# GpSimd's element work ahead of the feed-forward part handed to VectorE and ScalarE, and second buffers for two small tables

## The chip, the core and the metric

The kernel runs on one core of a Trainium2 chip. The time is the device time of one execution in microseconds; the profile is of one execution. The engines are named as in the profile: PE (TensorE matrix multiplies; PEld its weight loads), DVE (VectorE), ACT (ScalarE), POOL (GpSimd), and SP, which issues the DMAs. Each engine works through its own queue in order, and waits on semaphores of the others.

## The reference

One transformer layer over 2048 tokens of width 1024, all in float32:

```
mod = silu(c) @ w_ada + b_ada            # six vectors: shift, scale, gate, twice
h   = rmsnorm(x) * (1 + scale1) + shift1
p   = h @ w_in
y_a = spatial gating of 128-token chunks (gelu, rmsnorm, causal 128x128 mixing)
y_b = 6 stick-breaking heads: weight = sigmoid(z) * product of sigmoid(-z) behind it
y_c = 6 dilated heads (strides 1, 4, 16; 129 offsets), rotary q and k, softmax;
      the three groups are scaled by a softmax over their log sums
x   = x + (1 + gate1) * (concat(y_a, y_b, y_c) @ w_out)
h   = rmsnorm(x) * (1 + scale2) + shift2
up  = causal depthwise convolution, width 3, of h @ w_up
x   = x + (1 + gate2) * ((silu(gate half) * val half) @ w_down)
out = rmsnorm(x) * g_final
```

## The kernel before

Products are made exact enough by splitting each operand into a rounded high part and the remainder: `split` (L88) casts the source to the high tile (L70, L72 or L74, by engine) and subtracts (L78) for the low tile. Every matrix product is then three PE products (high by high, high by low, low by high). So each weight piece that lands from memory as `wraw` passes through one cast to `whi` and one subtraction to `wlo` before PE can use it; the same holds for normed activations (`ln_tmp`, `hh`, `hl`; in the feed-forward part `gh`, `gl`), for rotated queries and keys (`rot`), and for the output weights (`woraw`, `wo_hi`, `wo_lo`) and the concatenated heads (`yraw`, `yh`, `yl`).

The tokens are worked on in two chunks of 1024. A text of tokens, `ORDER`, says in which order the units are written: projections of the queries and keys, of the values, of the gating part, stick-breaking heads (`st`), dilated heads (`dil`), the vectors from `w_ada`, the output projection (`op`, `oa`). Units marked with a tilde are worked off piece by piece between the blocks of stick-breaking heads. The tile framework then orders all instructions by a simulated timeline of its own, so a change of an instruction's engine also changes the order that the other engines get.

Which engine does a split's cast or subtraction, or one of the other element operations, is read from the table `ENGINES`: a letter for each site (a ACT, v DVE, p POOL), or a string of letters taken in turn. `whi` and `wlo` are the input weights' casts and subtractions (`whi0` and `wlo0` those of the opening stretch), `hlo0` and `hlo` the activations' low parts, `rot1` to `rotlo` the rotary steps, `sgu1` to `sgulo` the gating steps, `wolo`, `ysc`, `ylo` those of the output projection. The site `beta` (a product on the way from DVE's scan to PE's transposes) is POOL's in both kernels, and so are the feed-forward sites `wulo`, `wdm`, `wdlo`, `gv`, `ghi`, `glo`.

A block of a stick-breaking head passes PE (`z`), ACT (two sigmoids, L539 and L540), DVE (scan `excl`, L545), POOL (`beta`), PE (transposes `tr`), ACT (`wh`), DVE (`wl`, L78) and PE again (`av`). A dilated head writes scores' maxima and sums into the table `stat` and the negated maxima into `mx`; at its end `stat` is stored to memory. `BUFS` gives each tag its number of buffers; tags that it does not name have one, as `stat` and `mx` here:

```
nc.vector.tensor_tensor_reduce(e[:, j, ks], z[:, j, ks], self.mask[:, ks], 0.125, -3.0e38,
                               ALU.add, ALU.max, stat[:, blk, 0:1])
...
self.load(sd.rearrange("(p r) s -> p r s", r=16), stat)
```

In the opening stretch DVE sums the rows of `w_ada` into `ada_acc` (L185, L187), quarter by quarter; after each quarter PE sums over partitions (`ada_ps`), DVE finishes the columns `cols` (L179 to L181), and only then can the activations of that quarter be normed and multiplied.

Of the kernel before, what the change touches and what calls it, by code (L numbers as in the profile page):

```python
# [43 lines left out]
class Kernel:  # L44
# [16 lines left out]
    def engine(self, site):  # L61

        turns = ENGINES.get(site, site)
        n = self.turn[site] = self.turn.get(site, -1) + 1
# [790 lines left out]
    def run(self):  # L855
        tc, nc, i = self.tc, self.nc, self.i
        self.constants()
        self.ps = _Bufs(self.pool("ps", space=PSUM), BUFS)
        self.p1 = _Bufs(self.pool("p1"), BUFS)
        self.pa = _Bufs(self.pool("pa", side="right"), BUFS)  # L860
        dr = self.dr
# [185 lines left out]
        for c, order in enumerate(ORDER):  # L1047
            u = units(c, hT[c])
            for token in order.split():
# [48 lines left out]
                elif what == "rel":  # L1098
                    finish()
                    self.p1.release()  # L1100
                    self.ps.release()
                    self.ps = _Bufs(self.pool("ps2", space=PSUM), {**BUFS, "gm": 2, "z": 3})
                    self.po = _Bufs(self.pool("po"), BUFS)
                elif what == "free":
                    finish()
                    self.pa.release()
                    self.pw = _Bufs(self.pool("pw", side="right"), BUFS)
                    self.pn = _Bufs(self.pool("pn", side="right"), BUFS)
# [41 lines left out]
        self.cp.release()  # L1150


ENGINES = {"whi0": "a", "wlo0": "pppv", "lnt0": "a", "hlo0": "pppv", "lnt": "va", "lnx00": "avv", "lnx01": "aav", "lnx10": "v", "lnx11": "v", "lnx": "va", "hlo": "pvv", "whi": "v", "wlo": "pvv", "qkhi": "avv", "qklo": "v", "cqk": "a", "rot1": "ppv", "rot2": "pv", "rot3": "v", "rothi": "aav", "rotlo": "pvv", "sgu1": "pv", "sgu2": "p", "sguhi": "ap", "sgulo": "ppv", "ya": "aaav", "fold": "a", "beta": "p", "whi_s": "a", "whi_d": "avv", "wom": "v", "wohi": "aav", "wolo": "pv", "ysc": "pv", "yhi": "av", "ylo": "pv", "wuhi": "v", "wulo": "pvv", "wdm": "p", "wdhi": "av", "wdlo": "ppv", "upc": "av", "gv": "pppv", "ghi": "ap", "glo": "ppv", "vhi": "av", "vlo": "v", "uc": "v"}

BUFS = {"gm": 3, "z": 2, "tr": 2, "av": 1, "wraw": 2, "whi": 3, "wlo": 3, "s8": 3, "cs": 2, "tmp2": 2, "khat": 3, "vhat": 2, "q": 2, "beta": 4, "excl": 3, "wh": 2, "wl": 2, "fold": 1, "ys": 1, "x4": 2, "yraw": 2, "ysc": 4, "yh": 2, "yl": 2, "xo": 3, "wuraw": 4, "wul": 3, "wuh": 3, "wdraw": 2, "fx": 2, "up": 3, "dn": 5, "wdh": 2, "wdl": 2, "upc": 3, "cv": 3, "gh": 4, "gl": 4, "fs": 4, "fry": 2, "frr": 2}

WOUT = 6
EARLY = (0, 1, 5, 6, 7)
# [39 lines left out]
```

## Time and profile before

| | us |
|---|---|
| median of 3 runs | 2798.26 (2794.84 to 2798.34) |
| the profiled execution | 2798.01 |
| its span, first to last instruction | 2796.3 |
| busy in the span: PE, DVE, ACT, POOL | 2641.1, 2122.0, 983.0, 1043.6 |

About the first 1200 us are the part ahead of the feed-forward part, with some 1400 us as the point from which nearly all work is feed-forward. An engine's idle time costs something only where PE ends up waiting for it. [...]

### The profile page before, as it was taken

How to read it: one execution, taken by the hardware profiler on the slowest of the kernel's cores; microseconds unless marked ns; L12 is line 12 of the kernel's file. 1: busy time of each engine (PE TensorE's matmuls, PEld its weight loads, DVE VectorE, ACT ScalarE, POOL GpSimd, SP SyncE). 2: the span in 40 equal slices, each digit the busy share in tenths (PEclk: the TensorE clock that was granted, in tenths of full speed). 3: DMA queues.
4: the chain of work that ended last, by engine and by line, in shares of the span. 5: the costliest groups of instructions: out<-in, count | busy, mean ns of one | idle time of the engine just before them, and what ended most of it. 6: DMA issues, size and time to landing. Idle time of an engine off the chain costs nothing.

```text
span 2796.3 us, 36851 instructions
## 1 busy us (share of the span) xinstructions
PE 2641.1 (94%) x13430; PEld 2210.9 (79%) x13430; DVE 2122.0 (76%) x3188; ACT 983.0 (35%) x1842; POOL 1043.6 (37%) x995
## 2 busy tenths in 40 slices
PE   6989899799988999999999999999998999999998
PEld 5878888788966777877788888888877888888886
DVE  5586878666588898855877777778788778777776
ACT  5244433333455677633221222121362112112114
POOL 3163413230037555423433334433444343333323
PEclk9999999899998999999999999999999999999999
DMA  7645485869665333186111111111232111111111
GB/s 236 194 126 165 153 267 163 216 169 232 169 167 158 99 91 95 54 270 241 59 45 46 46 46 53 49 50 53 68 106 98 53 50 49 48 50 46 46 38 61
DMA packets 305298, 309.38 MB, mean 111 GB/s; under 512 B 65517, under 2 KB 245597, under 8 KB 305117
## 3 DMA queue, kind: packets, MB, share of 16 engines
q1 hardware_dynamic: 305116, 307.02, 37.0%
q8 instruction: 107, 1.75, 0.3%
q14 instruction: 75, 0.61, 0.1%
HBM read 232.36 MB, written 68.30 MB: 108 GB/s over the span
## 4 chain that ended last, share of the span: by engine, by line
PE 61%; DVE 13%; DMA 9%; ACT 4%; issue 3%; POOL 1%; SPq 1%; DVEq 0%; POOLq 0%; ACTq 0%
PE up L93 11%; PE up L94 11%; PE up L92 11%; PE dn L94 5%; PE dn L92 5%; PE dn L93 5%; DVE excl L545 3%; PE gmv L342 3%; DMA wada<-in_w_ada_dram 2%; PE av L565 2%; DMA wraw<-in_w_in_dram 1%; DVE wl L78 1%; SPq L83 1%; PE tr L554 1%; PE op L102 1%
## 5 line engine op out<-in xcount | busy, mean ns | idle before, releaser
L92 PE MATMUL up<-gh,wuh 128*128 128x512 f32 x1408 | 553.5, 393 | 2.1 <-ACT gh L260 2.1
L94 PE MATMUL up<-gh,wul 128*128 128x512 f32 x1408 | 555.2, 394 | 0.0
L93 PE MATMUL up<-gl,wuh 128*128 128x512 f32 x1408 | 555.0, 394 | 0.0
L829 DVE TENSOR_TENSOR acc<-dn,acc 128x512 f32<-128x512 f32 x688 | 441.2, 681 | 102.3 <-PE dn L94 101.6
L787 DVE SCALAR_TENSOR_TENSOR cv<-upc,cw,cv 128x512 f32<-128x512 f32 x352 | 338.5, 962 | 104.7 <-ACT cv L785 101.5
L78 POOL TENSOR_TENSOR beta<-beta,excl 128x127 f32<-128x127 f32 (+2 forms) x240 | 258.4, 1080 | 290.6 <-DVE excl L545 259.9
L92 PEld LDWEIGHTS up<-gh,wuh 128*128 128x128 f32 x1408 | 265.1, 188 | 62.1 <-ACT gh L260 2.3
L93 PEld LDWEIGHTS up<-gl,wuh 128*128 128x128 f32 x1408 | 265.4, 189 | 61.4 <-issue 0.2
L94 PEld LDWEIGHTS up<-gh,wul 128*128 128x128 f32 x1408 | 265.2, 188 | 60.0 <-issue 0.2
L92 PE MATMUL dn<-wdh,gh 128*128 128x512 f32 x688 | 270.8, 395 | 11.7 <-DVE acc L829 10.4
L93 PE MATMUL dn<-wdl,gh 128*128 128x512 f32 x688 | 270.8, 394 | 0.0
L94 PE MATMUL dn<-wdh,gl 128*128 128x512 f32 x688 | 256.1, 395 | 0.0
L785 ACT ACTIVATE cv<-up,cb 128x512 f32<-128x512 f32 x176 | 136.6, 777 | 285.7 <-DVE upc L72 279.2
L545 DVE TENSOR_TENSOR_SCAN excl<-z,excl,beta 128x512 f32<-128x512 f32 x144 | 183.7, 1276 | 19.5 <-ACT z L540 17.1
L70 ACT ACTIVATE upc<-up 128x512 f32<-128x512 f32 x88 | 52.5, 597 | 379.3 <-PE up L94 379.2
L70 ACT ACTIVATE wh<-tr 128x128 fp32r<-128x128 f32 (+2 forms) x240 | 126.7, 535 | 164.6 <-PE tr L554 160.5
L72 DVE CAST wuh<-wuraw 128x512 fp32r<-128x512 f32 x176 | 131.4, 785 | 65.4 <-PE up L93 60.0
L78 DVE TENSOR_TENSOR wl<-tr,wh 128x128 fp32r<-128x128 f32 (+2 forms) x240 | 141.3, 594 | 39.7 <-ACT wh L70 39.6
L342 PE MATMUL gmv<-whi,hh 128*128 128x256 f32 x576 | 168.6, 294 | 2.8 <-DVE vst L78 2.8
L342 PE MATMUL gmv<-whi,hl 128*128 128x256 f32 x576 | 169.5, 296 | 1.0 <-DVE hl L78 0.9
L342 PE MATMUL gmv<-wlo,hh 128*128 128x256 f32 x576 | 167.6, 292 | 2.4 <-DVE wlo L78 2.4
L92 PEld LDWEIGHTS dn<-wdh,gh 128*128 128x128 f32 x688 | 129.9, 189 | 43.1 <-DVE acc L829 11.9
(252 smaller groups left out, 5764.1 us busy)
## 6 DMA issues: line engine op xcount, KB each, us to landing
wuraw<-in_w_up_dram SPq DMA_DIRECT2D x176, 256.0 KB, 3.1
wdraw<-in_w_down_dram SPq DMA_DIRECT2D x44, 512.0 KB, 3.6
wada<-in_w_ada_dram SPq DMA_DIRECT2D x32, 512.0 KB, 6.7
wraw<-in_w_in_dram SPq DMA_DIRECT2D x112, 128.0 KB, 4.5
vd<-vst SPq DMA_DIRECT2D x12, 1024.0 KB, 4.7
q<-bq SPq DMA_DIRECT2D x48, 256.0 KB, 4.2
q<-cq SPq DMA_DIRECT2D x48, 256.0 KB, 4.0
x<-xo SPq DMA_DIRECT2D x24, 512.0 KB, 5.0
```

The source lines that it names most:

```text
L70: self.nc.scalar.activation(out, in_, AF.Copy)
L72: self.nc.vector.tensor_copy(out, in_)
L78: (self.nc.vector if eng == "v" else self.nc.gpsimd).tensor_tensor(out=out, in0=a, in1=b, op=op)
L92: self.nc.tensor.matmul(ps, ah, bh, start=(k == 0), stop=False)
L93: self.nc.tensor.matmul(ps, ah, bl, start=False, stop=False)
L94: self.nc.tensor.matmul(ps, al, bh, start=False, stop=(k == n - 1))
L342: self.nc.tensor.matmul(ps[:, e, :], a[:, o:o + P], b, start=(n == 0), stop=(n == 3 * KB - 1))
L545: nc.vector.tensor_tensor_scan(x[:, x0:x0 + n][:, ::-1], z[:, :n][:, ::-1], b[:, :n][:, ::-1], before, op0=ALU.mult, op1=ALU.bypass)
L565: last = nc.tensor.matmul(av[:, q0:256], vhat[kc // 2][:, (kc % 2) * 4 + e, :], w[:, e, q0:256], start=(kc == top and m == 0), stop=(kc == ...
L785: nc.scalar.activation(t, ps, AF.Identity, bias=self.cb[:, blk:blk + 1], scale=self.cw[2][:, blk:blk + 1])
L787: nc.vector.scalar_tensor_tensor(out=t, in0=u[:, tap:tap + TG], scalar=self.cw[tap][:, blk:blk + 1], in1=t, op0=ALU.mult, op1=ALU.add)
L829: nc.vector.tensor_tensor(out=acc[t][:, ns], in0=ps, in1=acc[t][:, ns], op=ALU.add)
```

## The change

In `ENGINES` all sites that lie ahead of the feed-forward part and had a p are given to v (`sguhi` to a), but for `beta`. The cast `whi`, which was DVE's, is given to a. `hlo` is also used by the norm ahead of the feed-forward part. In `BUFS`, `stat` and `mx` get two buffers each. No other line differs.

```
-ENGINES = {... "wlo0": "pppv", ... "hlo0": "pppv", ... "hlo": "pvv", "whi": "v", "wlo": "pvv", ...
-  "rot1": "ppv", "rot2": "pv", ... "rotlo": "pvv", "sgu1": "pv", "sgu2": "p", "sguhi": "ap", "sgulo": "ppv", ...
-  "wolo": "pv", "ysc": "pv", ... "ylo": "pv", ...}
+ENGINES = {... "wlo0": "v", ... "hlo0": "v", ... "hlo": "v", "whi": "a", "wlo": "v", ...
+  "rot1": "v", "rot2": "v", ... "rotlo": "v", "sgu1": "v", "sgu2": "v", "sguhi": "a", "sgulo": "v", ...
+  "wolo": "v", "ysc": "v", ... "ylo": "v", ...}
-BUFS = {... "fold": 1, "ys": 1, "x4": 2, ...}
+BUFS = {... "fold": 1, "ys": 1, "stat": 2, "mx": 2, "x4": 2, ...}
```

By the built programs 117 of POOL's instructions go away (115 of them to DVE, two casts to ACT), and 76 casts go from DVE to ACT. DVE's 115 are 60 of 512 elements a row (35 `wlo`, 14 `hl`, 11 `gl`), 35 of 1024 (rotary, gating, four `wo_lo`, four `yl`) and 20 smaller ones (`yl` and `yraw`).

DVE in the opening stretch, from the second quarter of `w_ada` on, before the change (`cols_71` are the columns of that quarter):

```order
L187 SCALAR_TENSOR_TENSOR ada_acc<-wada,cact,ada_acc 128x512 x7
L78 TENSOR_TENSOR wlo<-wraw,whi 128x512
L185 TENSOR_SCALAR ada_acc<-wada,cact 128x512
L187 SCALAR_TENSOR_TENSOR ada_acc<-wada,cact,ada_acc 128x512 x6
L179 TENSOR_TENSOR cols_71<-ada_ps,cols 128x2
```

The same place after it:

```order
L187 SCALAR_TENSOR_TENSOR ada_acc<-wada,cact,ada_acc 128x512
L78 TENSOR_TENSOR wlo<-wraw,whi 128x512 x2
L187 SCALAR_TENSOR_TENSOR ada_acc<-wada,cact,ada_acc 128x512
L78 TENSOR_TENSOR hl<-ln_tmp,hh 128x512
L187 SCALAR_TENSOR_TENSOR ada_acc<-wada,cact,ada_acc 128x512
L78 TENSOR_TENSOR hl<-ln_tmp,hh 128x512
L187 SCALAR_TENSOR_TENSOR ada_acc<-wada,cact,ada_acc 128x512 x2
L78 TENSOR_TENSOR wlo<-wraw,whi 128x512 x2
L187 SCALAR_TENSOR_TENSOR ada_acc<-wada,cact,ada_acc 128x512
L78 TENSOR_TENSOR wlo<-wraw,whi 128x512
L185 TENSOR_SCALAR ada_acc<-wada,cact 128x512
L187 SCALAR_TENSOR_TENSOR ada_acc<-wada,cact,ada_acc 128x512 x3
```

The row of `cols_71` follows next. Five `wlo` and two `hl` stand among the sums now where one `wlo` stood, and the columns come behind 9 of the L187 sums instead of 13.

ACT in the first stick-breaking head (`beta` and `z` are the two sigmoids of a block, `wh` its transposed high part), before:

```order
L539 ACTIVATE beta<-z 128x128
L540 ACTIVATE z<-z 128x128
L70 ACTIVATE wh<-tr 128x2x128
L539 ACTIVATE beta<-z 128x256
L540 ACTIVATE z<-z 128x256
L70 ACTIVATE wh<-tr 128x3x128
L539 ACTIVATE beta<-z 128x512
L540 ACTIVATE z<-z 128x512
L70 ACTIVATE wh<-tr 128x4x128
```

And after:

```order
L539 ACTIVATE beta<-z 128x128
L540 ACTIVATE z<-z 128x128
L70 ACTIVATE whi<-wraw 128x512 x2
L70 ACTIVATE wh<-tr 128x2x128
L539 ACTIVATE beta<-z 128x256
L540 ACTIVATE z<-z 128x256
L70 ACTIVATE wh<-tr 128x3x128
L539 ACTIVATE beta<-z 128x512
L540 ACTIVATE z<-z 128x512
L70 ACTIVATE whi<-wraw 128x512 x2
L70 ACTIVATE wh<-tr 128x4x128
```

The casts of landed weights now stand in ACT's queue between the blocks' sigmoids and `wh`.

DVE where the output weights are made, beside the second chunk's stick-breaking heads (`gate_8353` is the gate, `yscale` the dilated heads' scale), before:

```order
L78 TENSOR_TENSOR woraw<-woraw,gate_8353 128x1024
L545 SCALAR_TENSOR_TENSOR excl<-z,excl,beta 128x512
L78 TENSOR_TENSOR yraw<-ycraw,yscale 128x4x64
L78 TENSOR_TENSOR wl<-tr,wh 128x4x128
L545 SCALAR_TENSOR_TENSOR excl<-z,excl,beta 128x512
L78 TENSOR_TENSOR wl<-tr,wh 128x4x128
L545 SCALAR_TENSOR_TENSOR excl<-z,beta 128x128
L78 TENSOR_TENSOR wo_lo_8374<-woraw,wo_hi_8373 128x1024
L78 TENSOR_TENSOR wl<-tr,wh 128x4x128
```

And after:

```order
L78 TENSOR_TENSOR woraw<-woraw,gate_8353 128x1024
L545 SCALAR_TENSOR_TENSOR excl<-z,excl,beta 128x512
L78 TENSOR_TENSOR yraw<-ycraw,yscale 128x4x64
L78 TENSOR_TENSOR wo_lo_8367<-woraw,wo_hi_8366 128x1024
L78 TENSOR_TENSOR wl<-tr,wh 128x4x128
L545 SCALAR_TENSOR_TENSOR excl<-z,excl,beta 128x512
L78 TENSOR_TENSOR wl<-tr,wh 128x4x128
L545 SCALAR_TENSOR_TENSOR excl<-z,beta 128x128
L78 TENSOR_TENSOR wo_lo_8374<-woraw,wo_hi_8373 128x1024
L78 TENSOR_TENSOR yraw<-ycraw,yscale 128x16x16
L78 TENSOR_TENSOR wl<-tr,wh 128x4x128
```

One more `wo_lo` and one more `yraw` stand ahead of the blocks' `wl` within these rows. PE's order in this stretch and behind it is nearly the same as before; in the first chunk and among the dilated heads it is mixed differently.

## Rows read from the trace of the kernel before

**Rows 1.** The page, first part: busy us, share of the span, instructions.
```profile
PE 2641.1 (94%) x13430; PEld 2210.9 (79%) x13430; DVE 2122.0 (76%) x3188; ACT 983.0 (35%) x1842; POOL 1043.6 (37%) x995
```

**Rows 2.** Stages; columns: length, PE, PEld, DVE, ACT, POOL busy, granted clock, DMA.
```profile
0.00:480.00 480.00, 427.70 (x2645) 380.63 (x2646) 347.13 (x496) 206.09 (x370) 172.79 (x170) 0.96 0.61 184
480.00:790.00 310.00, 279.29 (x1850) 253.80 (x1849) 204.12 (x506) 120.47 (x313) 48.35 (x31) 0.95 0.75 194
790.00:1190.00 400.00, 363.75 (x2105) 300.02 (x2104) 349.24 (x432) 255.94 (x533) 222.44 (x238) 0.96 0.39 111
1190.00:2796.00 1606.00, 1570.34 (x6836) 1276.49 (x6834) 1221.55 (x1756) 400.51 (x626) 600.03 (x557) 0.99 0.23 72
```

**Rows 3.** Waits of PE, 0 to 1400 us; columns: total us, times, longest.
```profile
PE av L565 <- DVE wl L78: 17.9, 16, 2.7
PE z L534 <- DVE excl L545: 17.2, 34, 2.0
PE zc L620 <- DVE stat L623: 11.6, 6, 4.8
```

**Rows 4.** Groups by form, 0 to 1400 us: count, busy us, mean ns, idle before.
```profile
L78 POOL TENSOR_TENSOR wlo<-wraw,whi 128x512 fp32r<-128x512 f32 x35 | 52.9, 1513 | 260.9 <-DVE whi L72 202.9 <-ACT whi L70 25.7 <-PE gm L317 13.9
L78 DVE TENSOR_TENSOR wlo<-wraw,whi 128x512 fp32r<-128x512 f32 x53 | 49.5, 944 | 8.0 <-ACT whi L70 7.0
L72 DVE CAST whi<-wraw 128x512 fp32r<-128x512 f32 x76 | 43.1, 588 | 39.3 <-DMA wraw<-in_w_in_dram 37.3 <-PE gm L316 0.9 <-PE gm L101 0.7
L187 DVE SCALAR_TENSOR_TENSOR ada_acc<-wada,cact,ada_acc 128x512 f32<-128x512 f32 x28 | 29.2, 1044 | 1.6 <-DMA wada<-in_w_ada_dram 1.0
L78 DVE TENSOR_TENSOR woraw<-woraw,gate 128x1024 f32<-128x1024 f32 x8 | 13.9, 1737 | 0.0
L70 ACT ACTIVATE whi<-wraw 128x512 fp32r<-128x512 f32 x12 | 7.3, 626 | 16.3 <-DMA wraw<-in_w_in_dram 16.2
```

**Rows 5.** Timeline of DVE, opening stretch: start, us, instruction, count.
```profile
10.92 0.75 DVE L187 SCALAR_TENSOR_TENSOR ada_acc<-wada,cact,ada_acc 128x512 f32<-128x512 f32 x1
...
20.29 11.06 DVE L187 SCALAR_TENSOR_TENSOR ada_acc<-wada,cact,ada_acc 128x512 f32<-128x512 f32 x7
31.27 0.68 DVE L78 TENSOR_TENSOR wlo<-wraw,whi 128x512 fp32r<-128x512 f32 x1
...
36.99 0.15 DVE L179 TENSOR_TENSOR cols<-ada_ps,cols 128x2 f32<-128x2 f32 x1
```

**Rows 6.** Stretches of 8 us, columns as in rows 2.
```profile
24.00:32.00 8.00, 6.26 (x25) 4.90 (x23) 7.86 (x7) 1.89 (x3) 6.02 (x4) 1.00 0.81 253
40.00:48.00 8.00, 8.00 (x25) 6.84 (x26) 6.88 (x11) 3.04 (x5) 2.96 (x3) 0.50 1.09 354
752.00:760.00 8.00, 6.73 (x34) 6.73 (x35) 3.15 (x16) 5.12 (x11) 1.07 (x1) 0.57 0.51 133
832.00:840.00 8.00, 4.82 (x19) 4.15 (x20) 8.00 (x9) 3.81 (x9) 7.00 (x6) 0.65 0.94 174
848.00:856.00 8.00, 6.65 (x26) 5.16 (x27) 8.00 (x10) 4.48 (x8) 6.96 (x6) 0.79 0.54 133
```

**Rows 7.** Timeline of all engines, 512 to 522 us, first dilated head.
```profile
515.93 1.23 DVE L78 TENSOR_TENSOR stage<-stage,cos 128x1024 f32<-128x1024 f32 x1 [2.62 <-DMA gate_acc<-ada_acc]
...
516.06 3.31 POOL L78 TENSOR_TENSOR stage<-stage,sin 128x1024 f32<-128x1024 f32 x1 [24.42 <-DMA gate_acc<-ada_acc]
...
517.08 2.57 DVE L72 CAST whi<-wraw 128x512 fp32r<-128x512 f32 x1
```

**Rows 8.** Waits of DVE, 0 to 1400 us, columns as in rows 3.
```profile
DVE whi L72 <- DMA wraw<-in_w_in_dram: 37.3, 17, 5.5
...
DVE ys L487 <- DMA yc<-ys: 22.5, 4, 8.5
...
DVE ec L623 <- DMA stat<-stat: 11.7, 4, 7.4
```

More of the change, by code (lines that the diff above doesn't have):

```diff
@@ L1150, in run @@
         self.cp.release()
-ENGINES = {"whi0": "a", "wlo0": "pppv", "lnt0": "a", "hlo0": "pppv", "lnt": "va", "lnx00": "avv", "lnx01": "aav", "lnx10": "v", "lnx11": "v", "lnx": "va", "hlo": "pvv", "whi": "v", "wlo": "pvv", "qkhi": "avv", "qklo": "v", "cqk": "a", "rot1": "ppv", "rot2": "pv", "rot3": "v", "rothi": "aav", "rotlo": "pvv", "sgu1": "pv", "sgu2": "p", "sguhi": "ap", "sgulo": "ppv", "ya": "aaav", "fold": "a", "beta": "p", "whi_s": "a", "whi_d": "avv", "wom": "v", "wohi": "aav", "wolo": "pv", "ysc": "pv", "yhi": "av", "ylo": "pv", "wuhi": "v", "wulo": "pvv", "wdm": "p", "wdhi": "av", "wdlo": "ppv", "upc": "av", "gv": "pppv", "ghi": "ap", "glo": "ppv", "vhi": "av", "vlo": "v", "uc": "v"}
-BUFS = {"gm": 3, "z": 2, "tr": 2, "av": 1, "wraw": 2, "whi": 3, "wlo": 3, "s8": 3, "cs": 2, "tmp2": 2, "khat": 3, "vhat": 2, "q": 2, "beta": 4, "excl": 3, "wh": 2, "wl": 2, "fold": 1, "ys": 1, "x4": 2, "yraw": 2, "ysc": 4, "yh": 2, "yl": 2, "xo": 3, "wuraw": 4, "wul": 3, "wuh": 3, "wdraw": 2, "fx": 2, "up": 3, "dn": 5, "wdh": 2, "wdl": 2, "upc": 3, "cv": 3, "gh": 4, "gl": 4, "fs": 4, "fry": 2, "frr": 2}
+ENGINES = {"whi0": "a", "wlo0": "v", "lnt0": "a", "hlo0": "v", "lnt": "va", "lnx00": "avv", "lnx01": "aav", "lnx10": "v", "lnx11": "v", "lnx": "va", "hlo": "v", "whi": "a", "wlo": "v", "qkhi": "avv", "qklo": "v", "cqk": "a", "rot1": "v", "rot2": "v", "rot3": "v", "rothi": "aav", "rotlo": "v", "sgu1": "v", "sgu2": "v", "sguhi": "a", "sgulo": "v", "ya": "aaav", "fold": "a", "beta": "p", "whi_s": "a", "whi_d": "avv", "wom": "v", "wohi": "aav", "wolo": "v", "ysc": "v", "yhi": "av", "ylo": "v", "wuhi": "v", "wulo": "pvv", "wdm": "p", "wdhi": "av", "wdlo": "ppv", "upc": "av", "gv": "pppv", "ghi": "ap", "glo": "ppv", "vhi": "av", "vlo": "v", "uc": "v"}
+BUFS = {"gm": 3, "z": 2, "tr": 2, "av": 1, "wraw": 2, "whi": 3, "wlo": 3, "s8": 3, "cs": 2, "tmp2": 2, "khat": 3, "vhat": 2, "q": 2, "beta": 4, "excl": 3, "wh": 2, "wl": 2, "fold": 1, "ys": 1, "stat": 2, "mx": 2, "x4": 2, "yraw": 2, "ysc": 4, "yh": 2, "yl": 2, "xo": 3, "wuraw": 4, "wul": 3, "wuh": 3, "wdraw": 2, "fx": 2, "up": 3, "dn": 5, "wdh": 2, "wdl": 2, "upc": 3, "cv": 3, "gh": 4, "gl": 4, "fs": 4, "fry": 2, "frr": 2}
 WOUT = 6
```

## The prediction

> **What bounds the kernel now.** I read the page's first part, then stage sums, then who waits for whom, then the places where PE is slow. PE is busy for 94% of the span [rows 1]: it bounds the kernel, and only its idle time and its slow clock can be won back. By stages it idles 480 - 427.7 = 52 us in the first, 31 us among the dilated heads, 36 us in the second chunk's heads and 36 us in all that follows [rows 2]. The granted clock is 0.95 to 0.96 in the first three and 0.99 behind them. So the change works on 1190 us that hold 119 us of idle PE. The longest items of PE's waits there are all on DVE: `wl` 17.9 us, the scan `excl` 17.2 us, the maxima of the dilated heads 11.6 us [rows 3]. POOL is no item of weight, though its share is a third. It counts only through what it does to DVE.
>
> What it does shows in DVE's own rows. In the opening stretch one sum into `ada_acc` took 0.75 us; the seven sums from 20.29 us on took 11.06, which is 1.58 each [rows 5], while POOL was busy 6.02 of 8 us [rows 6]. A `wlo` on DVE took 0.68 us in a quiet moment [rows 5], but 0.944 on average [rows 4]. A rotary product of 1024 elements took 1.23 us, and the cast behind it 2.57, under a POOL product of 3.31 [rows 7]. So DVE and POOL hold each other up when both work on operands in SBUF, and POOL's 1.513 us for a `wlo` [rows 4] buy nothing where DVE has such work as well.
>
> [...]
>
> **The change part by part.** The sum goes against the profiled execution, 2798.01 us (span 2796.3, 1.7 around it). The median of the runs is 2798.26, so the same number serves.
>
> *DVE's load.* Added: 60 subtractions of 512 elements at 0.68 = 41 us [rows 5], 35 of 1024 at 1.23 = 43 us [rows 7], 20 smaller ones at 0.68 at most = 14 us. That is 98. Removed: 76 casts at 0.588 = 45 us [rows 4]. Relieved, since POOL keeps only `beta`: 53 x (0.944 - 0.68) = 14 us on `wlo`, 28 x (1.044 - 0.75) = 8 on the sums, 8 x (1.737 - 1.23) = 4 on `woraw` [rows 4, 5, 7]. That is 26 of these three groups alone. So DVE carries at most 98 - 45 - 26 = 27 us more in 1400, and its chains get shorter, for POOL's 1.5 us becomes 0.68.
>
> *Opening stretch.* DVE does 9 sums (0.75 less some overlap, say 0.67) and 7 subtractions (0.6 pitched) where 13 sums, slowed, and one subtraction stood: 6.0 + 4.2 + 0.4 = 10.6 us from 20.3 on, so the columns of the second quarter come at about 31 instead of 36.99 [rows 5]. DMA is at 0.81 and more there [rows 6], so the weights may be late next. [...] I take 4 us won. Bounds: 8 won (6 of lead and some of the clock), 3 lost (the subtractions delay the sums).
>
> *Two tables of maxima and sums.* The next head's maxima no longer wait until the last head's table has landed. DVE waited 11.7 us for that in four places, 7.4 at the longest [rows 8], and PE 4.8 at that one [rows 3], with a clock of 0.57 behind it [rows 6], which is 8 x 0.43 = 3.4 us. I take 6 us won, bounds 12 and 0. Late next is `ys`, which still has one buffer (22.5 us of DVE [rows 8]).
>
> *Other casts and subtractions up to 790 us.* PE's waits on `wl` and `excl` come to 35 us [rows 3], part of it behind instructions stretched as above or behind a `beta` that stood in POOL's queue behind a 2 to 3 us product [rows 7]. I take a good quarter, 10 us won, which is nearer to the unstretched rows than to none. Bounds: 20 won, and 9 lost, if a third of DVE's 27 us more reaches PE.
>
> *Casts to ACT.* 76 x 0.626 = 48 us more on ACT [rows 4], which is busy 206 of 480 and 120 of 310 us [rows 2], so the work itself hides in its idle time. The wait does not: a cast that waits for its weights at the head of the queue now holds back the sigmoids and `wh` behind it, where it held back DVE before (37.3 us, 17 times, 5.5 at the longest [rows 8]). DVE is freed of the same wait, except where the `wlo` behind it comes at once. I take 3 us lost; bounds 0 and 37.
>
> [...]
>
> *Output weights and projection, 790 to 1190.* Here DVE is already full, 349 of 400 us, with 8.00 of 8 in two stretches in which PE idles and has a clock of 0.65 and 0.79 [rows 2, 6]. Four `wo_lo` and four `yl` at 1.23, four shorter `yl` and the `yraw` add some 15 us; POOL's side was slowing DVE, 4 us on `woraw` alone, and the same again on other SBUF work there as I judge it. The block's `beta` meets an empty queue. I take 1 us lost; bounds 4 won and 9 lost.
>
> *Behind 1190 us.* 11 `gl` and some `yl`, some 10 us of DVE in 1606 in which PE idles 36: nothing, bounds 3 either way.
>
> Sum: -4 - 6 - 10 + 3 + 1 = -16, so 2798 - 16 = 2782 us. With likely errors of each term, 2768 to 2794.
>
> **Rivals.**
> *More opens up.* If waits on `wl` and `excl` go almost wholly (-30 instead of -10) and the clock stays at 1.00 where it fell, some 38 us are won: 2760. For it: DVE stands behind all three of PE's large items. Against: ACT's 0.6 us steps and DVE's scan stay as they are.
> *The idle time only moves.* PE's order in the first two stages is mixed anew, `ys` still stalls DVE, `beta` is still POOL's and still slows DVE, so wins and losses cancel: 2797. For it: POOL was hardly ever what PE waited for. [...]
> *ACT stands still for weights (slower).* The place is the casts ahead of the sigmoids in the heads and units of the first 790 us. If three quarters of the 37 us reach PE, that is 28 lost instead of 3; with the two load terms at half (-10), 2798 + 28 - 10 - 4 = 2812. It decides from about 19 us of such waits on, where it eats what the rest wins. For it: SP issues in order, and weights came late 17 times. Against: raw buffers come free sooner, with the subtraction no longer waiting for POOL. [...]
> *DVE is full in the heads of the second chunk (slower).* If all 15 us added there reach PE and little is relieved: 2798 + 9 + 3 - 5 = 2805.
>
> **How the numbers follow.** Forecast 0.53, more opens up 0.14, only moves 0.16, ACT stands still 0.12, DVE full 0.05. What this kernel's measurement can tell from no change is 0.2%, 5.6 us. The forecast's own range lies below 2792.7 for the most part: faster 0.53 x 0.92 + 0.14 + a fifth of "only moves" = 0.66. Slower is the two slow rivals and a tail of the moving one, 0.17; the rest, 0.17, is no change. The range 2755 to 2808 takes in the forecast, the fast rival, the moving one, and the DVE one; it leaves out half of the ACT one and the ends.
>
> **What would show it.** DVE's `wlo` at 0.68 to 0.75 on average and the sums near 0.75; the second quarter's columns near 31 us; POOL's 444 us in the first 1190 [rows 2] down by over 100, all but `beta` gone; no wait of DVE for the table's landing; PE's waits on `wl`, `excl` and the maxima together 25 to 35 us instead of 47. The forecast is wrong if ACT's waits for `wraw` exceed 30 us with PE waiting on `z`, `wh` or `wlo` behind them, if PE's idle time between 790 and 1190 rises above 40 us, or if PE's first 790 us idle as long as before (83 us) though DVE's rows got short.

## The result and the profile after

The changed kernel takes 2768.48 us at the median (2762.24 to 2772.08, 4 runs) against 2796.55 for the kernel before beside it: ratio 0.9899, interval 0.9886 to 0.9912. It is 28 us faster; 16 were forecast. The profiled execution took 2772.08, with a span of 2770.4; it is the slowest of the four.

The page's first part, as in [rows 1]:

```profile
PE 2626.6 (95%) x13430; PEld 2201.3 (79%) x13430; DVE 2109.4 (76%) x3227; ACT 1025.6 (37%) x1918; POOL 857.5 (31%) x878
```

PE did the same 13430 products in 2626.6 us instead of 2641.1. So 14.5 of the span's 25.9 us are shorter busy time for the same products, and 11.4 are idle time. The stages, with the columns of [rows 2]:

```profile
0.00:480.00 480.00, 434.46 (x2704) 387.06 (x2705) 341.51 (x522) 236.68 (x422) 78.72 (x113) 0.97 0.65 196
480.00:790.00 310.00, 283.72 (x1928) 257.76 (x1927) 205.37 (x525) 147.31 (x367) 22.37 (x22) 0.97 0.76 195
790.00:1190.00 400.00, 360.46 (x2070) 298.16 (x2070) 349.17 (x426) 249.70 (x516) 184.52 (x207) 0.97 0.40 112
1190.00:2770.00 1580.00, 1547.95 (x6732) 1258.32 (x6732) 1213.37 (x1757) 391.92 (x613) 571.87 (x536) 0.99 0.22 70
```

The clock, given as a share of full speed, stands at 0.97 in all three early stages, where it was 0.96, 0.95 and 0.96. Part of the 14.5 us is this clock: PE was busy for 96.6 us at half clock (0.50) in the whole span before and for 77.4 after. I estimate this at (96.6 - 77.4) / 2 = 9.6 us, with half the clock taken as half the work; in the kernel before, products of 128x512 began every 0.43 us at a clock of 0.50 (45 to 48 us) and every 0.23 at 1.00 (51 to 52). What the other 5 us are, no view shows. POOL's work before 1190 fell from 444 to 286 us. DVE's sum is hardly changed: it took over 115 instructions and gave up 76 casts. Its groups between 0 and 1400 us and one of ACT's, as in [rows 4]:

```profile
L78 DVE TENSOR_TENSOR wlo<-wraw,whi 128x512 fp32r<-128x512 f32 x88 | 60.2, 700 | 63.4 <-ACT whi L70 63.1
L70 ACT ACTIVATE whi<-wraw 128x512 fp32r<-128x512 f32 x88 | 52.9, 626 | 127.0 <-DMA wraw<-in_w_in_dram 92.5 <-PE gm L101 17.3 <-DMA ck<-rot 6.9
L187 DVE SCALAR_TENSOR_TENSOR ada_acc<-wada,cact,ada_acc 128x512 f32<-128x512 f32 x28 | 20.8, 747 | 0.3
L78 DVE TENSOR_TENSOR woraw<-woraw,gate 128x1024 f32<-128x1024 f32 x8 | 12.4, 1545 | 0.0
```

A `wlo` fell from 944 to 700 ns and a sum from 1044 to 747, so 88 `wlo` now cost DVE 60 us where 53 cost 50. DVE's opening stretch, as in [rows 5]:

```profile
19.65 0.75 DVE L187 SCALAR_TENSOR_TENSOR ada_acc<-wada,cact,ada_acc 128x512 f32<-128x512 f32 x1
20.32 1.28 DVE L78 TENSOR_TENSOR wlo<-wraw,whi 128x512 fp32r<-128x512 f32 x2
...
28.36 2.19 DVE L187 SCALAR_TENSOR_TENSOR ada_acc<-wada,cact,ada_acc 128x512 f32<-128x512 f32 x3
31.60 0.16 DVE L179 TENSOR_TENSOR cols<-ada_ps,cols 128x2 f32<-128x2 f32 x1 [1.05 <-PE ada_ps L177]
```

The columns of the second quarter come at 31.60 instead of 36.99. PE's waits up to 1400 us, as in [rows 3]:

```profile
PE z L534 <- DVE excl L545: 31.0, 37, 4.5
PE av L565 <- DVE wl L78: 17.7, 17, 2.6
PE trc L635 <- ACT ec L632: 14.1, 8, 7.5
```

Those on DVE's scan rose from 17.2 to 31.0, and on the maxima 3.0 of 11.6 are left. So the named waits did not shrink in sum, although PE idled less: rows of waits tell where PE stood, not what the change won. The two instructions that PE waits for most had not been stretched in the first place, as `wl` shows, before and after:

```profile
L78 DVE TENSOR_TENSOR wl<-tr,wh 128x512 fp32r<-128x512 f32 x168 | 113.1, 676 | 36.1 <-ACT wh L70 35.9
L78 DVE TENSOR_TENSOR wl<-tr,wh 128x512 fp32r<-128x512 f32 x168 | 113.0, 674 | 26.5 <-ACT wh L70 26.5
```

The scans of 512 took 1.28 us in both kernels.

To see where the time came from, each kernel is cut at PE rows that it has in the same number: the end of the opening (32nd `ada_ps`), the first `gate_ps` (the gate ahead of the output weights), the 800th `tr` (near the end of the second chunk's stick-breaking heads), and the 2064th `dn` near the end of the feed-forward part. Start times in us of these rows:

| kernel | opening | gate | tr 800 | dn 2064 | gate to tr 800 |
|---|---|---|---|---|---|
| before | 56.6 | 821.5 | 1175.6 | 2771.6 | 354.1 |
| changed | 53.9 | 788.2 | 1152.0 | 2745.7 | 363.8 |
| rotary and gating sites alone | 53.9 | 797.3 | 1149.6 | 2745.2 | 352.4 |
| weights' sites alone | 54.8 | 805.0 | 1156.8 | 2751.9 | 351.8 |
| changed, output sites back | 56.1 | 787.2 | 1140.9 | 2737.8 | 353.7 |
| that, with two casts on ACT | 55.1 | 789.3 | 1136.2 | 2728.2 | 346.9 |

PE starts the same number of products between these cuts in both kernels. Up to the gate the change won 33.3 us; up to the 800th `tr` 9.7 of these were lost again; behind it 2.3 were won. Each row is one execution, and differences of up to 3 us say little: the changed kernel and the two in the last rows have the same sites ahead of the gate, and take 734.3, 731.1 and 734.2 us from the end of the opening to it.

### The profile page after: what moved, and what is told of

Read it like the earlier page. It is cut to its first block, busy times and chain, and to the rows that moved or that the text cites. A ratio compares the mean times of both kernels' runs of the same rounds, so it can differ in the third digit from the quotient of the medians.

```text
span 2770.4 us, 36801 instructions
## 1 busy us (share of the span) xinstructions
PE 2626.6 (95%) x13430; PEld 2201.3 (79%) x13430; DVE 2109.4 (76%) x3227; ACT 1025.6 (37%) x1918; POOL 857.5 (31%) x878
## 4 chain that ended last, share of the span: by engine, by line
PE 65%; DVE 14%; DMA 10%; ACT 6%; issue 3%; SPq 1%; POOL 0%; DVEq 0%; ACTq 0%; POOLq 0%
PE up L94 11%; PE up L93 11%; PE up L92 11%; PE dn L94 5%; PE dn L92 5%; PE dn L93 5%; DVE excl L545 3%; DMA wraw<-in_w_in_dram 2%; PE gmv L342 2%; DMA wada<-in_w_ada_dram 2%; PE av L565 2%; DVE wl L78 1%; PE gm L100 1%; PE tr L554 1%; PE gm L101 1%
## 5 line engine op out<-in xcount | busy, mean ns | idle before, releaser
L78 POOL TENSOR_TENSOR beta<-beta,excl 128x127 f32<-128x127 f32 (+2 forms) x240 | 267.5, 1116 | 869.6 <-DVE excl L545 758.5
L92 PEld LDWEIGHTS dn<-wdh,gh 128*128 128x128 f32 x688 | 129.8, 189 | 42.6 <-DVE acc L829 11.6
```

Source lines behind the costliest of these rows:

```text
L78: (self.nc.vector if eng == "v" else self.nc.gpsimd).tensor_tensor(out=out, in0=a, in1=b, op=op)
L92: self.nc.tensor.matmul(ps, ah, bh, start=(k == 0), stop=False)
```

## The experiments

Medians in us, and the ratio to the kernel before that ran beside it:

| run | median | ratio, interval |
|---|---|---|
| e1_tables | 2799.46 | 1.001, 1.000 to 1.002 |
| e2_no_tables | 2776.28 | 0.9932, 0.9919 to 0.9945 |
| e3_casts_dve | 2771.81 | 0.9908, 0.9889 to 0.9926 |
| e4_output_back | 2762.76 | 0.9884, 0.9868 to 0.9899 |
| p1_busy_pool | 2777.18 | 0.9925, 0.9903 to 0.9947 |
| p2_pool_work | 2788.48 | 0.9971, 0.9958 to 0.9984 |
| s1_weights | 2779.21 | 0.9938, 0.9923 to 0.9954 |
| s2_rotary_gating | 2773.46 | 0.9924, 0.9907 to 0.9941 |
| p3_rotary_beside | 2781.06 | 0.9937, 0.9923 to 0.9950 |
| p4_weights_beside | 2776.59 | 0.9916, 0.9903 to 0.9930 |
| e6_heads_act | 2753.45 | 0.9840, 0.9823 to 0.9857 |
| e7_output_back_no_tables | 2766.92 | 0.9890, 0.9877 to 0.9904 |

### The two tables

```
before + "stat": 2, "mx": 2                 (e1_tables)
changed - "stat": 2, "mx": 2                (e2_no_tables)
```

> The kernel before with one edit: two buffers each for the tables of maxima and sums; every engine site as before. Theory (the gain of 28 us comes from ending the mutual blocking of DVE and POOL, the tables are a side term): the forecast's own term, 6 us won, about 2790, range 2784 to 2797; DVE's wait for the table's landing (11.7 us) gone, sums and subtractions on DVE as slow as before (wlo mean above 0.9 us). Rival (the tables carry the gain, by letting PE's order among the dilated heads run on): 2780 or lower, with nothing changed in DVE's instruction times.

> The changed kernel with one edit: the two tables have one buffer again; all engine sites as in the change. Theory (blocking): most of the gain stays, about 2774, range 2770 to 2779, the waits for the table's landing back at 8 to 12 us on DVE. Rival (the tables carry the gain): 2785 or higher.

Alone the tables won nothing: 2799.46, 0 to 0.2% slower. Sums and subtractions on DVE stayed slow (`wlo` 932 ns). The waits moved, as e1's rows of PE between 0 and 1400 us show:

```profile
PE avc L658 <- DVE ys L487: 7.3, 2, 6.7
...
PE zc L620 <- DVE stat L623: 6.0, 3, 3.0
```

Of the 11.6 us behind the maxima [rows 3] 5.6 went, and 7.3 behind `ys` came in their place, the buffer that the prediction had named as late next. Without the tables the changed kernel keeps 20 us of its gain, so the rival is out. How much the tables bring there stays open: by medians 7.8 us, with intervals that lie clear of each other, but the profiled executions took 2771.93 without and 2772.08 with them, although the waits were back:

```profile
PE zc L620 <- DVE stat L623: 9.3, 7, 3.1
DVE ec L623 <- DMA stat<-stat: 18.4, 4, 7.5
```

### The parts alone

```
before + "wlo0", "hlo0", "hlo", "wlo": "v", "whi": "a"                        (s1_weights)
before + "rot1".."rot3", "rotlo", "sgu1", "sgu2", "sgulo": "v", "sguhi": "a"  (s2_rotary_gating)
```

> The kernel before with a part of the change: subtractions of input weights and of normed activations to DVE, casts of input weights to ACT; rotary, gating and output sites and the one-buffer tables as before. Theory (blocking on these sites carries most): 2778 to 2786. Rival (the dilated heads' rotary and gating steps carry most, since PE gained 34 us between 477 and 673 us): 2790 to 2797.

> The kernel before with the other part: rotary and gating steps to DVE (the gating cast to ACT), all else as before. Theory (weights' sites carry most): 2790 to 2797. Rival (rotary and gating carry most: POOL's 3.31 us product beside DVE's 2.57 us cast): 2778 to 2786.

Both parts are large: 17 us by the weights' sites, 23 by rotary and gating, with intervals that overlap. The second was more than either side had expected, and that with one buffer for each table. Together they would be 40; e7 below is just these two parts together and won 31, so they overlap by some 9. DVE's casts show the relief in s2, where they are still DVE's (between 0 and 1400 us):

```profile
L72 DVE CAST whi<-wraw 128x512 fp32r<-128x512 f32 x76 | 36.0, 498 | 41.8 <-DMA wraw<-in_w_in_dram 39.8 <-PE gm L101 1.0 <-PE gm L316 0.9
```

They took 498 ns instead of 588 [rows 4]. In the kernel before, 48 of the 76 had no POOL work beside them and took 422 ns on the mean, the other 28 took 873; s2 takes the products of 1024 away from POOL.

### The casts on ACT

```
changed, "whi": "v"                         (e3_casts_dve)
```

> The changed kernel with one edit: the 76 casts of input weights are DVE's again. Theory A (as forecast, the move to ACT is a small loss of about 3 us, since a cast that waits for its weights holds back sigmoids): 2765, with DVE's waits for the weights back at 30 us or more. Theory B (ACT takes 45 us off a DVE that stands behind PE's three largest waits): slower, 2774 to 2785, with PE's waits on wl and excl and the opening columns later.

The time lies between the two theories, and its interval overlaps that of the changed kernel. So the forecast's loss of 3 us is neither shown nor excluded. ACT did wait 92.5 us for weights in the changed kernel (the `whi` row above), but PE's longest wait did not come from it: up to 790 us PE waits 17.2 us on the scan in the changed kernel and 16.9 with the casts back on DVE.

### Is it the mutual blocking?

Each of the next four adds idle work on POOL to the changed kernel, on a scratch tile that nobody reads. The orders of DVE and ACT in the traces are the changed kernel's, and PE's too (but for 64 of 13430 places in p2), so their cuts compare directly with the changed kernel's.

```
p1: opening, per sum: 2nd quarter 3 products, 3rd 3 copies, 4th 3 memsets, 128x224 each
    g.tensor_tensor(out=j, in0=j, in1=j, op=ALU.mult) / g.tensor_copy(j, j) / g.memset(j, 0.0)
p2: for each step taken from POOL: ceil(n / 224) such products
p3, p4: behind the step, floor(n / 224) subtractions, the first reading the step's result o
    g.tensor_tensor(out=j[:, 0:w], in0=o[:, 0:w], in1=o[:, 0:w], op=ALU.subtract)
    p3 at rotary and gating steps, p4 at subtractions of weights and activations
```

> The changed kernel with idle work added on POOL in the opening stretch, on a scratch tile of 128 x 224 that nobody else reads: beside each sum into ada_acc of the second quarter three products with two inputs, of the third three copies, of the fourth three memsets. Every other engine's order is that of the changed kernel. Theory (DVE and POOL hold each other up on operands in SBUF, two-input sums too): sums of 512 beside POOL's products at 1.4 to 1.6 us instead of 0.75, beside copies between, beside memsets near 0.75; the columns of the second quarter later by 2 us or more, the total 0 to 6 us up. [...]

> The changed kernel, with every subtraction, rotary or gating step that the change took from POOL done on DVE as in the change, and beside it a product of about the same size on POOL on a scratch tile that nobody else reads. The order of DVE and ACT is that of the changed kernel, PE's too but for some 26 rows; POOL is loaded about as before the change up to 790 us. Theory (the gain is the end of the mutual blocking and of beta's queue): slower than the changed kernel by a third of the gain or more, 2778 to 2792, with DVE's wlo mean back at 0.85 us or more and PE's waits on wl and excl up. Rival (the gain comes from the shorter steps themselves, 0.7 us on DVE for 1.5 on POOL, and the order that the framework makes of them): 2766 to 2774.

> The changed kernel; behind each rotary or gating step that the change took from POOL, POOL does a subtraction of about the same size, whose first piece reads the step's result (so that it runs at that time) and writes a scratch tile that nobody reads. The orders of PE, DVE and ACT are those of the changed kernel. Theory (the dilated heads' part of the gain, 25 us between their first scores and the gate, is the end of blocking): that stretch back from 319 us to 328 or more, total 2778 to 2790. Rival (it is the shorter steps on the way, 3.31 us on POOL against 1.23 on DVE, and the order that follows from them): the stretch within 3 us of 319, total 2766 to 2774.

> The changed kernel; behind each subtraction of input weights or normed activations that the change took from POOL, POOL does a subtraction of about the same size, whose first piece reads the step's result and writes a scratch tile that nobody reads. The orders of PE, DVE and ACT are those of the changed kernel. Theory (blocking): DVE's wlo mean back from 0.70 to 0.78 us or more, the end of the opening stretch 2 us or more later, total 2773 to 2784. Rival (shorter steps and order): total 2766 to 2772.

The clearest rows are p4's. DVE in its opening stretch:

```profile
22.20 1.04 DVE L202 SCALAR_TENSOR_TENSOR ada_acc<-wada,cact,ada_acc 128x512 f32<-128x512 f32 x1
23.16 1.04 DVE L78 TENSOR_TENSOR hl<-ln_tmp,hh 128x512 fp32r<-128x512 f32 x1
24.13 1.04 DVE L202 SCALAR_TENSOR_TENSOR ada_acc<-wada,cact,ada_acc 128x512 f32<-128x512 f32 x1
...
34.97 0.15 DVE L194 TENSOR_TENSOR cols<-ada_ps,cols 128x2 f32<-128x2 f32 x1
```

and POOL's at the same time:

```profile
21.80 0.89 POOL L91 TENSOR_TENSOR junk<-wlo 128x224 f32<-128x224 f32 x1
22.77 0.89 POOL L93 TENSOR_TENSOR junk<-junk 128x224 f32<-128x224 f32 x1
23.73 0.89 POOL L91 TENSOR_TENSOR junk<-wlo 128x224 f32<-128x224 f32 x1
```

The two engines take turns, one instruction each every 0.96 us: a sum of 0.75 us takes 1.04, and POOL's piece 0.89, where it takes 0.56 with DVE idle (at 55.76 us); so each takes some 0.3 us longer than alone. The second quarter's columns slip from 31.60 back to 34.97. So the delay grew with the partner's instruction: pieces of 224 cost DVE 0.3 us each, POOL's `wlo` of 512 cost it 0.83 (1.58 in [rows 5] less 0.75), and its product of 1024 turned a cast, 0.42 us on the mean of the 48 with no POOL work beside them, into one of 2.57 [rows 7].

In p1 the scheduled pieces ran ahead of the sums that they were meant for. DVE beside copies, and then beside memsets:

```profile
31.48 0.85 DVE L201 SCALAR_TENSOR_TENSOR ada_acc<-wada,cact,ada_acc 128x512 f32<-128x512 f32 x1
...
45.72 3.89 DVE L201 SCALAR_TENSOR_TENSOR ada_acc<-wada,cact,ada_acc 128x512 f32<-128x512 f32 x5
```

POOL at those times:

```profile
24.85 17.84 POOL L193 COPY junk<-junk 128x224 f32<-128x224 f32 x24
42.75 8.34 POOL L195 MEMSET junk<- 128x224 f32 x24
```

A sum took 0.85 us beside copies and 1.4 to 1.6 nowhere; five in a row took 3.89 beside memsets, where the changed kernel with nothing on POOL took 3.90, so a memset cost nothing here. As to the 1.4 to 1.6, the expectation had taken the price of POOL's 512 columns for pieces of 224. Still DVE's instructions slowed down beside products (a `wlo` took 0.91 us, where it took 0.69 in the changed kernel) and copies, though no DMA was changed. The opening ended at 59.2 instead of 53.9; the median is 9 us up, but its interval overlaps the changed kernel's, and the profiled executions differ by 4.

The totals: p4 8 us slower than the changed kernel, p3 13, p2 20, all in the ranges of the theory. The intervals of p3 and p2 lie clear of the changed kernel's, p4's overlaps it. But `wlo` slowed less than the theory said (0.737 us in p4, 0.812 in p2), and p2's waits on `wl` and `excl` did not rise. There are three reservations. First, p2's POOL ran early and did more than before the change in the first 480 us, as its row with the columns of [rows 2] shows (281.52 us against 172.79):

```profile
0.00:480.00 480.00, 427.40 (x2651) 380.16 (x2652) 360.46 (x506) 235.04 (x418) 281.52 (x396) 0.96 0.61 186
```

Of the 13.9 us between p2's profiled execution and the changed kernel's, 9.7 arose in the opening, which ended at 63.6, later than in the kernel before, and 4.1 between the opening and the gate.

Second, in p3 the place was another than the theory's: from the dilated heads' first scores to the gate it took 321.4 us, 2.3 more than the changed kernel, as the rival had said; its loss lies ahead, among rotary and gating steps of the first 480 us.

Third, work on POOL delays more than DVE: a `beta` stands behind it in POOL's own queue. The 80 `beta` ahead of the gate start 27.5 us in all after their scans have ended in the kernel before, 8.0 in the changed one, 7.3 in p4, 19.0 in p3 and 51.6 in p2. So p4's loss holds none of this and p3's holds some. In the same way the gain of s1 (26.9) holds none, and that of s2 (11.7) may hold some. No run separates blocking from this queue at the rotary and gating sites.

Between the opening and the gate p3 lost 8.8 us and p4 5.1, of the 30.6 that the change won there (764.9 to 734.3). So idle work on POOL takes back some 14 of the 30.6, by single executions of which p4's is hardly beyond the 3 us named above. That is an estimate of what blocking and `beta`'s queue have together: small pieces block less than what they stand for (two of 0.3 us for a subtraction of 512 that cost 0.83, four for a product of 1024 that cost 2.57 - 0.42 = 2.15). Shorter steps on the way (1.23 us on DVE for 3.31 on POOL) and the other order that follows from them are left for the rest. These last two were not told apart.

### The second chunk's heads

```
changed, "wolo", "ysc", "ylo": "pv"                            (e4_output_back)
that, "wohi": "a", "yhi": "a"                                  (e6_heads_act)
e4_output_back - "stat": 2, "mx": 2                            (e7_output_back_no_tables)
```

> The changed kernel with one edit: the low parts of the output weights, the heads' scaling and their low parts alternate between POOL and DVE again, as before the change. Between the gate and the last stick-breaking transposes of the second chunk PE lost 9.7 us against the kernel before. Theory (DVE is full there, and the 15 us added to it reach PE): the 9.7 us come back in good part, 2758 to 2764, PE idle in that stretch below 33 us instead of 38.7. Rival A (these instructions on POOL block DVE as elsewhere): 2770 to 2776. Rival B (the loss stems from the weights of that stretch or from the order of the work, not from these sites): 2767 to 2770, idle time unchanged.

> The changed kernel with the three output sites alternating between POOL and DVE again, as in the run of that name, and two more edits of the same kind: the casts of the output weights and of the concatenated heads all on ACT, which is busy 254 of 400 us there, where DVE is busy 342. Theory (DVE bounds the second chunk's heads): 2757 to 2762, less idle PE than 30.5 us between the gate and the last transposes of the second chunk. Rival (waits there come from the chain of a block, not from DVE's load): 2762 to 2766.

> The changed kernel with the three output sites alternating between POOL and DVE again, and one buffer for each of the two tables. It asks for the sign of the tables' part, which came out as 0 to 3 us lost in the kernel before and some 8 us won in the changed one. Theory (a wait for the table's landing is 9 to 12 us of PE's waits, and half of it is won): 2767 to 2773, against 2763 with two buffers. Rival (the wait hides behind other work among the dilated heads, and the difference was the order's): 2759 to 2766.

The output sites given back make 2762.76, in the theory's range; the interval still overlaps that of the changed kernel, but the stretch shows it: from the gate to the 800th `tr` it takes 353.7 us again, with 30.5 of PE idle instead of 38.7. PE's order differs from the changed kernel's in only 103 of 13430 places, all in one stretch behind the gate. The other runs agree, each by one execution. The six kernels that divide these sites between POOL and DVE as before (before, e1, s1, s2, e4, e7) take 351.8 to 354.2 us from the gate to the 800th `tr`, with DVE busy for 314 to 317. The seven that have them on DVE (changed, e2, e3, p1 to p4) take 361.1 to 366.7, with DVE busy for 328 to 330. `beta` starts sooner behind its scan in the seven (26 to 28 us in all, against 38 to 43), and still they are slower: the load on DVE decides here. The stage's row, of the changed kernel, is above (DVE 349.17); of e6:

```profile
790.00:1190.00 400.00, 366.22 (x2119) 305.06 (x2118) 337.96 (x415) 263.04 (x533) 217.97 (x232) 0.97 0.43 121
```

DVE is down to 337.96 and PE idles 33.8 of these 400 us instead of 39.5. By the cuts the stretch takes 346.9 us, with DVE busy for 309.3 and PE idle for 27.4, against 30.5 in e4. e6 is the fastest of all, 2753.45, 45 us under the kernel before beside it and better than its own theory's 2757 to 2762; its interval lies clear of e4's. PE's waits in it, between 790 and 1190 us, with `wl` at 8.0 where the changed kernel had 17.0 and e4 12.7:

```profile
PE z L534 <- DVE excl L545: 11.7, 23, 1.6
PE av L565 <- DVE wl L78: 8.0, 11, 1.8
```

e7 came out 4 us over e4 with intervals that overlap, and between its two theories, so it does not settle the tables' part either: 0 to 3 us lost alone, 4 to 8 won beside the rest.

## Why the prediction was right in sign and short in size

The measured 2768.48 lies at the lower edge of the forecast's own range, 2768 to 2794, and nearer to the 2760 of the rival "more opens up" than to the 2782 of the forecast. Against the profiled execution before (2798.01 to 2772.08, 25.9 us), by the cuts:

| part | forecast | measured |
|---|---|---|
| opening stretch | -4 | -2.7 |
| tables, other casts and subtractions, casts to ACT (to the gate) | -6 - 10 + 3 = -13 | -30.6 |
| output weights and projection (gate to tr 800) | +1 | +9.7 |
| behind | 0 | -2.3 |

The stretch up to the gate won some 16 us more than forecast, the next one lost some 9 more. That these two errors have opposite signs, and so leave the sum no more than 10 to 12 us from the forecast, is luck.

**Opening stretch, -4: right at the columns, not shown at its end.** No run shows the 4 us as such, a choice between the bounds of 8 won and 3 lost; of the clock, the traces show 0.50 from 40 to 48 us before [rows 6], and 0.78 there but 0.50 from 48 to 56 after, where it was 0.91 before. The columns came at 31.60, where 31 were forecast, and the sums at 0.747. The lead of 5 us was gone one quarter on: eight subtractions now stood among DVE's sums between these columns and the next, DVE waited 1.33 us for weights, and the third quarter's columns came at 47.14 instead of 44.82, with PE waiting 4.2 us for them. At the stretch's end 2.7 were left in these two executions, but that is no more than their scatter: with the old sites of the opening (before, e1, s2) it ends at 53.9 to 56.6, with the new ones (changed, e2, e3, e4, e6, e7, s1) at 53.9 to 56.3. The bound of 3 lost (subtractions delay the sums) had named what took the lead away.

**"Other casts and subtractions up to 790 us", -10: the term that was mis-sized.** With the terms beside it, it stands for the 30.6 us measured where 13 were forecast. Two things were wrong in it. The sum counted PE's waits on `wl` and `excl` alone, 35 us, and took a quarter; these waits rose to 49, and the gain came elsewhere. The rotary and gating steps, 23 us by themselves in s2, stand in front of other work, and of other waits that went (PE's for the landing of rotated queries, 3.0 us up to the gate before, 0 after). And busy time counts too: up to the gate PE's idle time fell from 89.6 to 71.8 us, which is 17.8 and about what the terms up to there promised (17), but its busy time fell too, from 731.9 to 716.3, for the same products. Of these 15.6 us the clock accounts for 9.5 (54 us of PE's busy time at half clock before, 35 after); the other 6 stay open. In the sum the clock stood only in the opening's bound and as a few us beside the tables. The rival "more opens up" had this clock, but its condition, that the waits on `wl` and `excl` go almost wholly, did not come about.

**Two tables, -6: open.** Alone they brought nothing, which is the forecast's bound of 0; beside the rest they brought 4 to 8 us by medians, and nothing between the profiled executions.

**Casts to ACT, +3: open, and small at most.** By medians the move won 3 us instead (e3), within the scatter. DVE's waits for weights turned into ACT's, 92.5 us, far over the 30 that were named as a danger, but PE's waits on the scan up to 790 us are the same with the casts on DVE. The "ACT stands still" rival fell with that.

**Output weights, +1: past its bound of +9.** The load was counted as 15 us of DVE and set against relief of POOL's blocking, 4 us on `woraw` alone and as much again elsewhere. The relief on `woraw` was 8 x (1.737 - 1.545) = 1.5 us: four of the eight, each begun 0.2 to 0.9 us into a `beta` on POOL, still took 1.70 to 2.11 us, the other four 1.19 to 1.21. DVE's busy time between the cuts rose by 13.5 us and the stretch by 9.7. The place is just behind the gate, where the changed kernel's DVE is busy all of 40 us and PE idles 9.5 at a clock of 0.87 (columns of [rows 2]):

```profile
800.00:840.00 40.00, 30.47 (x146) 23.51 (x145) 40.00 (x45) 19.97 (x39) 22.30 (x15) 0.87 0.60 158
```

This was the mechanism of the rival "DVE is full in the heads of the second chunk", which came true in its place and was outweighed.

**Signs.** Came true: `wlo` 0.70, sums 0.747, POOL down by 158 us, no wait of DVE for the table's landing. Did not: PE's waits on `wl`, `excl` and the maxima are 52 us instead of 25 to 35. And PE idles 39.5 us between 790 and 1190, just short of the 40 named as the danger (36 before).

## What to carry to other kernels

Work that is split between VectorE and GpSimd can lose where the two hold each other up: look in the trace how long each instruction gets beside the partner's (0.75 us became 1.04 to 1.58 here beside subtractions and 0.85 beside copies), and whether the chain is then longer than on one engine. Price a stop of TensorE twice where the trace shows a lower clock behind it, as here (0.50 from 48 to 56 us in the changed kernel, behind a wait of 4.2 us): as its idle time and as the slow products (11.4 us measured, 9.6 estimated). And move such work by stages: where VectorE was already full, the same sites were better left divided (e4), and their casts given to ScalarE (e6).

## What the runs showed that was not expected

DVE and POOL alternated instruction by instruction in p4, 0.96 us a pair with pieces of 224, so short instructions on POOL held DVE up too, each for 0.3 us where a `wlo` of 512 did so for 0.83. A copy on POOL held a sum of 0.75 us up to 0.85, a memset not at all (five sums in 3.89 us, 3.90 without). And of the 28 us won, 20 were lost again (p2) by work whose result nobody read: an engine that is idle 69% of the span was not free.
